# Reordered first loads, a second column of its own, and bias rows in four column groups

## The chip, the cores and the metric

The kernel runs on one core of a Trainium2 chip. The metric is the device time of one execution in microseconds, as the median of several runs. All data are float32. Large products are made of three matmuls each: an operand is split into a high part (rounded for TensorE's float32r) and a low part (the rest), and high x high, low x high and high x low are summed.

## The reference

One transformer block over 1024 tokens of width 1024: an adaptive norm whose shift, scale and gate come from a small vector c, a projection into eight heads of dilated attention and eight heads of a gated delta rule, an output projection, and a gated feed-forward layer. What the change touches is the beginning:

```
c_act = silu(c)
mod = c_act @ w_ada + b_ada                      # 6 x 1024
sh1, sc1, g1, sh2, sc2, g2 = split(mod, 6)
h = rmsnorm(x, norm_attn_g) * (1.0 + sc1) + sh1
proj = h @ w_in                                  # q, k, v, z, b, a
...
bias = rel_bias[bucket(steps * dilation)]        # 32 buckets x 8 heads, added to the attention scores
```

## The kernel before

Channels lie on partitions. The 1024 channels of x are eight blocks of 128 (blocks 0 to 7 here; block 0 is the first); block k of x is `xts[k]`, 128 x 1024 tokens. `mod` is kept as 48 columns of 128: columns 0 to 7 are sh1, columns 8 to 15 are sc1, and so on. The gate of block k is `G1[:, k] = (1 + mod[:, 8+k]) * ga[:, k]`, with ga the norm's weights; so block k of x can only be scaled when column 8+k of mod is known.

The first stage projects x by 512 columns of w_in (`wfirst`), before the norm's division by the root mean square is known; that is multiplied in later. For each block k:

- ScalarE casts the weights `wf[k]` to their high part `wh_f` (L343) and GpSimd makes the low part `wl_f` (L344).
- ScalarE scales x by G1 into the high part `hh[k]`, in two halves of 512 tokens (L359), and VectorE makes the low part `hl[k]` (L360).
- TensorE adds three matmuls of 512 columns for each of six PSUM banks, f0 to f5 (L247): eighteen matmuls for a block. Banks 0 to 3 want the first half of the tokens, 4 and 5 the second.
- For the norm, ScalarE squares x (L303), and TensorE sums the squares in one bank (`sums`, L305) and multiplies x by the scaled columns for beta and a (`wbg`, L295) in another (`sums2`, L309). Both use four groups of 32 output columns, one after the other, so that four small matmuls share the array.

Blocks 0 to 4 go in that order; of blocks 5 to 7 the six banks are finished bank by bank later (`first_end`).

The columns of mod are sums over the eight blocks of c (`rows4`, L206): for each block four calls of TensorE, one for each group of 32 output partitions. VectorE transposes the result (L214) and adds b_ada (L218). Column 8 has a load of its own, `wa8`, in two halves; the others come in groups, `groups = ((9, 3), (12, 4), (0, 4), (4, 4))`: first column and count. Group 0 (columns 9 to 11) is summed in the middle of block 0, after bank 3; group 1 in block 3; groups 2 and 3 after block 4. A group's weights come in four loads into four buffers (tag `qk`), so loads of a group wait until TensorE has read the one before.

The bias rows (L188) are a product of a 33 x 8 matrix (`rb`: the 32 rows of rel_bias and a row of ones) and a 33 x 1344 table of zeros and ones, in three matmuls of 448 columns with 8 output rows, each into a bank of its own; VectorE negates them into `Rs` (L193). They are stored to DRAM much later (L377), and attention reads them there. They are bound to come after the sum of column 8 on TensorE, and block 0 after them.

All loads are issued by SyncE (SP) in one queue, in the order of the program. The vector c (`cc`), rel_bias, the table (two loads), b_ada (`bada`) and the norm's weights (`ga`) are six small loads ahead of x. Instructions of an engine run in the order in which the program's scheduler put them.

## Time and profile before

| | |
|---|---|
| median of three runs | 1336.08 us |
| lowest, highest run | 1334.43, 1340.38 us |
| the profiled execution | 1336.0 us, span 1334.3 us |
| busy share of the span | PE 98%, DVE 63%, ACT 46%, POOL 18% |
| moved by DMA | 236.82 MB, mean 177 GB/s |

In the profile PE is TensorE's matmuls, PEld its weight loads, DVE is VectorE, ACT is ScalarE, POOL is GpSimd and SPq the issuing of loads and stores by SyncE. A row of the timeline has the start and the length in microseconds, the engine, the line of the kernel, the operation, out<-in by the names of the tiles, and the count; in brackets the idle time of the engine before it and what ended that. A float32 matmul is listed as two records, so 32 calls count as 64. Busy times of the stretches are per engine, followed by the granted clock of TensorE, the share of the sixteen DMA engines and the rate.

### The profile page before, as it was taken

The page shows a single profiled execution, that of the slowest core. Times are in us where ns is not written, and L with a number is a line of the kernel's source. Part 1 is how long each engine was busy: PE and PEld are TensorE (multiplying, and loading weights), DVE is VectorE, ACT ScalarE, POOL GpSimd, SP SyncE. Part 2 cuts the span into 40 slices and gives each one's busy share as a digit, 9 for nine tenths or more (in the row PEclk, how much of TensorE's full clock was granted, in tenths as well). Part 3 has the DMA queues.
Part 4 walks back from the last instruction along what each step waited for, and adds up shares of the span by engine and source line. Part 5 has one row for each costly group of instructions (what it writes and reads, how often), then busy time and mean ns, then how long its engine had stood idle before and what let it go on. Part 6 is the DMA issues. An engine that isn't in the chain of part 4 may idle for free.

```text
span 1334.3 us, 25026 instructions
## 1 busy us (share of the span) xinstructions
PE 1306.8 (98%) x9440; PEld 1066.4 (80%) x9440; DVE 836.2 (63%) x1609; ACT 618.6 (46%) x1238; POOL 236.7 (18%) x241
## 2 busy tenths in 40 slices
PE   8999999999999999999999999999999999999997
PEld 5777797889988877677778788888888888888876
DVE  3685775566946122555289967576766676474597
ACT  4397614337232343544487433333333333444555
POOL 2344503334213432343510000000000000000000
PEclk9999999999999999999999999999999999999999
DMA  8625665466452565763744545364445656666685
GB/s 325 224 70 175 180 206 173 135 201 196 131 155 65 138 158 149 214 189 105 235 154 130 169 152 199 108 209 137 158 150 166 213 205 216 227 222 197 201 266 196
DMA packets 188520, 236.82 MB, mean 177 GB/s; under 512 B 48494, under 2 KB 96079, under 8 KB 188400
## 3 DMA queue, kind: packets, MB, share of 16 engines
q1 hardware_dynamic: 181488, 228.94, 54.4%
q10 hardware_dynamic: 6912, 6.29, 1.4%
q8 instruction: 74, 1.21, 0.4%
q14 instruction: 46, 0.38, 0.1%
HBM read 172.37 MB, written 62.92 MB: 176 GB/s over the span
## 4 chain that ended last, share of the span: by engine, by line
PE 77%; DVE 8%; DMA 7%; ACT 3%; issue 2%; POOL 2%; SPq 1%; ACTq 0%; POOLq 0%; DVEq 0%
PE wua L1686 9%; PE wga L1686 9%; PE X L1888 7%; PE wo L592 6%; PE wuc L1686 4%; PE wgc L1686 4%; PE g_a L592 4%; PE Z L1888 4%; PE f L247 2%; PE wgb L1686 2%; PE Y L1888 2%; PE wub L1686 2%; DVE tm L908 2%; DVE tt L912 2%; PE tr L1399 2%
## 5 line engine op out<-in xcount | busy, mean ns | idle before, releaser
L1676 DVE TENSOR_TENSOR wl_db<-wr_db,wh_db 128x512 fp32r<-128x512 f32 x77 | 52.9, 690 | 67.5 <-ACT wh_db L1675 67.2
L1675 ACT CAST wh_db<-wr_db 128x512 fp32r<-128x512 f32 x77 | 47.5, 622 | 87.3 <-PE X L1888 37.8
L1373 DVE CUSTOM_DVE_ANT_0 X<-S,bt 128x128 f32<-128x128 f32 (+7 forms) x64 | 30.9, 517 | 68.9 <-PE S L1368 43.6
L1888 PE MATMUL X<-wl_db,wh_da 128*128 128x512 f32 x160 | 62.4, 390 | 0.3 <-DVE wl_db L1676 0.3
L1888 PE MATMUL X<-wh_db,wl_da 128*128 128x512 f32 x160 | 62.3, 389 | 0.0
L1888 PE MATMUL X<-wh_db,wh_da 128*128 128x512 f32 x160 | 62.3, 389 | 0.0
L1377 ACT ACTIVATE X<-X,sc 128x128 f32<-128x128 f32 (+7 forms) x64 | 37.0, 579 | 41.0 <-DVE sc L1373 40.9
L1676 DVE TENSOR_TENSOR wl_da<-wr_da,wh_da 128x512 fp32r<-128x512 f32 x77 | 52.8, 686 | 2.1 <-ACT wh_da L1675 2.1
L592 PE MATMUL wo<-yh,wh_wo 128*128 128x512 f32 x128 | 53.4, 417 | 0.1
L1675 ACT CAST wh_da<-wr_da 128x512 fp32r<-128x512 f32 x77 | 47.5, 617 | 12.2 <-PE wua L1686 5.8
L1379 POOL TENSOR_SCALAR X<-X,sc 128x128 f32<-128x128 f32 (+7 forms) x64 | 35.8, 567 | 94.3 <-DVE sc L1378 91.8
L592 PE MATMUL g_a<-hh,wh_a 128*128 128x512 f32 x128 | 51.2, 400 | 0.0
L592 PE MATMUL wo<-yh,wl_wo 128*128 128x512 f32 x128 | 51.1, 400 | 0.0
L592 PE MATMUL wo<-yl,wh_wo 128*128 128x512 f32 x128 | 50.8, 397 | 0.3 <-DVE yl L1506 0.3
L592 PE MATMUL g_a<-hl,wh_a 128*128 128x512 f32 x128 | 50.3, 393 | 0.0
L592 PE MATMUL g_a<-hh,wl_a 128*128 128x512 f32 x128 | 50.1, 391 | 0.0
L1675 ACT CAST wh_wg_s<-wg_s 128x512 fp32r<-128x512 f32 x33 | 20.6, 623 | 57.6 <-PE wuc L1686 24.3
L1675 ACT CAST wh_wu_s<-wu_s 128x512 fp32r<-128x512 f32 x33 | 20.4, 621 | 44.1 <-PE wga L1686 17.2
L1675 ACT CAST wh_wg<-wr_wg 128x512 fp32r<-128x512 f32 x31 | 19.2, 622 | 46.5 <-PE wua L1686 18.9
L618 PE MATMUL g_va<-wh_va,hh 128*128 128x256 f32 x128 | 38.2, 298 | 0.0
L618 PE MATMUL g_va<-wl_va,hh 128*128 128x256 f32 x128 | 38.2, 298 | 0.0
L618 PE MATMUL g_va<-wh_va,hl 128*128 128x256 f32 x128 | 37.8, 296 | 0.0
(552 smaller groups left out, 4138.6 us busy)
## 6 DMA issues: line engine op xcount, KB each, us to landing
wm<-in_wada SPq DMA_DIRECT2D x44, 512.0 KB, 4.9
wr_da<-ao_d SPq DMA_DIRECT2D x77, 256.0 KB, 2.8
wr_wu<-in_wu SPq DMA_DIRECT2D x50, 256.0 KB, 2.8
wr_wg<-in_wg SPq DMA_DIRECT2D x48, 256.0 KB, 3.2
ao_d<-a SPq DMA_DIRECT2D x44, 256.0 KB, 2.9
wr_wd<-in_wdn SPq DMA_DIRECT2D x44, 256.0 KB, 2.8
wr_db<-wt_d SPq DMA_DIRECT2D x44, 256.0 KB, 2.6
ao_d<-as SPq DMA_DIRECT2D x33, 256.0 KB, 2.0
```

Source lines behind the costliest of these rows:

```text
L247: nc.tensor.matmul(first[bank], a[:, w0], b[k][:, cs], start=(k == 0 and n_ == 0), stop=(k == KT - 1 and n_ == 2))
L592: last[0] = nc.tensor.matmul(ps, a[:, w0], b[k0 + k4][:, cs], start=(i == 0), stop=(i == n - 1))
L618: last[0] = nc.tensor.matmul(ps[:, :n], a[k][:, ts_], b[:, w0], start=(i == 0), stop=(i == 23))
L908: nc.vector.tensor_tensor(out=tv, in0=bc(nt[:, j, j + 1 : 32], j + 1), in1=tt[:, j, 0 : j + 1].unsqueeze(1).to_broadcast([P, m, j + 1]), o ...
L912: nc.vector.tensor_tensor(out=tt[:, j + 1 : 32, 0 : j + 1], in0=tt[:, j + 1 : 32, 0 : j + 1], in1=tv, op=ALU.add)
L1373: nc.vector.tensor_tensor_reduce(out=x[:, 0:w], in0=pss[e][:, 0:w], in1=bt[:, e, 480 - w : 480], scale=1.0, scalar=3e38, op0=ALU.add, op1= ...
L1377: nc.scalar.activation(x[:, 0:w], x[:, 0:w], AF.Exp, scale=-1.0, bias=sc[:, 0:1], accum_out=sc[:, 2:3])
L1379: nc.gpsimd.tensor_scalar(out=x[:, 0:w], in0=x[:, 0:w], scalar1=sc[:, 3:4], scalar2=0.0, op0=ALU.mult, op1=ALU.add)
L1675: nc.scalar.copy(hi, src)
L1676: (eng or nc.vector).tensor_tensor(out=lo, in0=src, in1=hi.bitcast(F32), op=ALU.subtract)
L1686: nc.tensor.matmul(ps, a[:, w0], b, start=(first and k == 0 and n_ == 0), stop=(k == 3 and n_ == 2), skip_group_check=True,)
L1888: nc.tensor.matmul(bank[b], a[:, ts_], w, start=(first and n_ == 0), stop=(last and n_ == 2), skip_group_check=True,)
```

## The change

The change rewrites the beginning of the first stage:

- b_ada, the norm's weights and c come in one load, `pk` (128 x 64), between the two halves of column 8's weights. The silu reads c from there.
- Then come w of block 0, x of block 0 in two halves of 512 tokens, the weights of column 9 (`wa[1]`, two halves), x and w of block 1, wba, group 0, the table, and from x of block 2 on the rest as before.
- Column 9 is a group of its own (group 4), summed in block 0 after bank 3; group 0 is now columns 10 and 11, in two loads, and is summed in block 1 after bank 2. The scaled columns `wbg` of blocks 0 and 1 are made together, in block 1.
- The bias rows are four matmuls of 336 columns, one in each group of 32 output columns, all in the first 336 columns of the bank `sums2`. One VectorE instruction negates all four, one memset clears the bank again. They stand in block 1, after bank 2, and block 0 no longer waits for them. rel_bias is now part of the table. Four stores take the place of three.
- The table's two tiles move from buffers with the tag `qd` to `kt`.

The core of the diff:

```diff
-    nc.sync.dma_start(cc[:, 0:KT], I["cc"])
-    nc.scalar.activation(cc[:, 0:KT], cc[:, 0:KT], AF.Silu)
-    rb = const([33, 8], "rb")
-    nc.vector.memset(rb[32:33, :], 1.0)
-    tbl = start("tbl", "qd", [33, 896]), start("tbl2", "qd", [33, 448])
-    wa8 = start("wa8", "qk", [P, KT, P])
...
+    pk = const([P, 64], "pk")
+    wa = [start(f"wa{j}", "qk", [P, KT, P]) for j in range(2)]
+    wa_load(0, 0)
+    nc.sync.dma_start(pk, I["pk"])
+    wa_load(0, 1)
+    nc.scalar.activation(cc[:, 0:KT], pk[:, 56:64], AF.Silu)
+    bada, ga = pk[:, 0:48], pk[:, 48:56]
+    tbl = start("tbl", "kt", [33, 672]), start("tbl2", "kt", [33, 704])
...
-    def bias_rows(behind):
-        for j in range(3):
-            n = 448
-            ps = tbank(f"ps_R{j}")
-            with tc.issue_after(behind[0].ins):
-                mm = nc.tensor.matmul(
-                    ps[:8, 0:n], rb, tbl[j // 2][:, n * (j % 2) : n * (j % 2) + n], start=True, stop=True
-                )
-            Rs = start(f"Rs{j}", "tc", [8, HALF])
-            with tc.issue_after(behind[1].ins):
-                nc.vector.tensor_scalar(out=Rs[:, 0:n], in0=ps[:8, 0:n], scalar1=-1.0, scalar2=None, op0=ALU.mult)
-            Rss.append(Rs)
-        return mm
+    Rs = start("Rs", "tc", [P, HALF])
+    def bias_rows():
+        ps = aux2[:, 0:336]
+        for j in range(4):
+            nc.tensor.matmul(
+                ps[32 * j : 32 * j + 32], tbl[1][:, 672:704], tbl[j // 2][:, 336 * (j % 2) : 336 * (j % 2) + 336],
+                start=False, stop=True, skip_group_check=True,
+            )
+        nc.vector.tensor_scalar(out=Rs[:, 0:336], in0=ps, scalar1=-1.0, scalar2=None, op0=ALU.mult)
+        nc.vector.memset(ps, 0.0)
...
-    groups = ((9, 3), (12, 4), (0, 4), (4, 4))
+    groups = ((10, 2), (12, 4), (0, 4), (4, 4), (9, 1))
...
-    x_load(0)
     w_load(0)
+    for hf in range(2):
+        x_load(0, slice(hf * HALF, (hf + 1) * HALF))
+    for i in range(2):
+        wa_load(1, i)
+    x_load(1)
+    w_load(1)
+    nc.sync.dma_start(wba, I["wba"])
     mod_load(0)
-    nc.sync.dma_start(wba, I["wba"])
-    for k in range(1, 4):
+    nc.sync.dma_start(tbl[0], I["tbl"][:, 0:672])
+    nc.sync.dma_start(tbl[1], I["tbl"][:, 672:1376])
+    for k in range(2, 4):
         x_load(k)
         w_load(k)
...
             for bank in range(6):
-                with tc.issue_after(mm.ins) if (k, bank) == (0, 0) else ExitStack():
-                    first_mm(bank, k)
+                first_mm(bank, k)
                 if (k, bank) == (0, 3):
+                    with tc.issue_after(newest[0].ins):
+                        mod_sum(4)
+                if (k, bank) == (1, 0):
+                    scaled(0, 2)
+                if (k, bank) == (1, 2):
+                    bias_rows()
                     mod_sum(0)
```

The queue of SP, from its first load on, before (wa is column 8's weights, xt is x, wf is w, wm is group 0):

```order
L170 DMA wa_121<-in_wa 128x512
L162 DMA cc<-in_cc 128x8
L170 DMA wa_121<-in_wa 128x512
L171 DMA rb<-in_rel 32x8
L173 DMA tbl<-in_tbl 33x896
L173 DMA tbl_120<-in_tbl 33x448
L119 DMA bada<-in_bada 128x48
L119 DMA ga<-in_ga 128x8
L257 DMA xt_154<-in_xT 128x1024
L260 DMA wf_148<-in_wfirst 128x512
L270 DMA wm_0_168<-in_wada 128x2x384
L270 DMA wm_1_170<-in_wada 128x2x384
```

and with the change (wa_116 is column 8, wa_117 column 9; the lines are those of the changed kernel):

```order
L166 DMA wa_116<-in_wa 128x512
L169 DMA pk<-in_pk 128x64
L166 DMA wa_116<-in_wa 128x512
L254 DMA wf_142<-in_wfirst 128x512
L251 DMA xt_148<-in_xT 128x512 x2
L166 DMA wa_117<-in_wa 128x512 x2
L251 DMA xt_149<-in_xT 128x1024
L254 DMA wf_142<-in_wfirst 128x512
L327 DMA wba<-in_wba 128x256
L265 DMA wm_0_168<-in_wada 128x4x256
L265 DMA wm_1_170<-in_wada 128x4x256
L329 DMA tbl<-in_tbl 33x672
```

The first loads of w and x move from ninth and tenth place to fourth to sixth, and x and w of block 1 ahead of group 0; the table moves behind it.

TensorE up to block 0, before (ps_R are the bias rows, f_138 to f_140 the first three banks, hh_93 and hl_101 block 0 of x):

```order
L206 MATMUL sums<-wa_121,cc 32x32 x32
L188 MATMUL ps_R_260<-tbl,rb 8x448
L188 MATMUL ps_R_264<-tbl,rb 8x448
L188 MATMUL ps_R_268<-tbl_120,rb 8x448
L247 MATMUL f_138<-hh_93,wh_f_219 128x512
L247 MATMUL f_139<-hh_93,wh_f_219 128x512
L247 MATMUL f_140<-hh_93,wh_f_219 128x512
L247 MATMUL f_138<-hh_93,wl_f_220 128x512
```

and with the change (f_132 to f_137 are the six banks):

```order
L200 MATMUL sums<-wa_116,cc 32x32 x32
L241 MATMUL f_132<-hh_93,wh_f_216 128x512
L241 MATMUL f_133<-hh_93,wh_f_216 128x512
L241 MATMUL f_134<-hh_93,wh_f_216 128x512
L241 MATMUL f_135<-hh_93,wh_f_216 128x512
L241 MATMUL f_136<-hh_93,wh_f_216 128x512
L241 MATMUL f_137<-hh_93,wh_f_216 128x512
L241 MATMUL f_132<-hh_93,wl_f_217 128x512
```

The bias rows are gone from here, and six high x high matmuls instead of three stand ahead of the first one that wants the low part of the weights.

TensorE in the middle of block 1 with the change (f_134 and f_135 are its third and fourth bank, hh_94 and hl_102 block 1 of x, wm group 0):

```order
L241 MATMUL f_134<-hh_94,wh_f_315 128x512
L241 MATMUL f_134<-hh_94,wl_f_316 128x512
L241 MATMUL f_134<-hl_102,wh_f_315 128x512
L200 MATMUL sums<-wm_0_168,cc 32x64 x16
L200 MATMUL sums<-wm_1_170,cc 32x64 x16
L241 MATMUL f_135<-hh_94,wh_f_315 128x512
L241 MATMUL f_135<-hh_94,wl_f_316 128x512
L184 MATMUL sums_139<-tbl,tbl_123 32x336 x2
L184 MATMUL sums_139<-tbl_123 32x336 x2
L241 MATMUL f_135<-hl_102,wh_f_315 128x512
```

Before, block 1 held projection matmuls alone, and group 0 was summed in block 0, after the fourth bank; that place now has column 9. The order of the instructions behind the first stage is the same, but for some rows of the second projection's beginning.

## The prediction

> **What bounds the kernel now.** I read the page first, then the stretches of the span, then the waits, then the first 60 us in order of time. The page and two stretches (microseconds, then each engine's busy time, the granted TensorE clock, DMA share, GB/s):

> ```profile
> PE 1306.8 (98%) x9440; PEld 1066.4 (80%) x9440; DVE 836.2 (63%) x1609; ACT 618.6 (46%) x1238; POOL 236.7 (18%) x241
> ...
> 0.00:20.00 20.00, 15.59 (x172) 8.36 (x176) 7.97 (x25) 6.29 (x11) 3.13 (x14) 1.00 0.82 295
> 20.00:60.00 40.00, 39.78 (x358) 27.56 (x348) 20.14 (x31) 21.88 (x34) 12.29 (x10) 1.00 0.79 294
> ```

> TensorE is busy 98% of the span and is the bound. It lacks 4.4 us in the first 20 and 0.2 us in the next 40. So the first stage can lose or gain time only up to about 26 us; behind that its matmuls follow one another.

> The opening, in order of time (start, length, engine, line, what; in brackets the idle time before it and its releaser):

> ```profile
> 1.79 0.43 SPq L170 DMA_DIRECT2D wa<-in_wa  x1
> ...
> 3.93 0.21 ACT L163 ACTIVATE cc<-cc 128x8 f32<-128x8 f32 x1 [1.62 <-DMA cc<-in_cc]
> ...
> 3.94 0.43 SPq L119 DMA_DIRECT2D ga<-in_ga  x1
> ...
> 4.19 0.66 PE L206 MATMUL sums<-wa,cc 128*32 128x32 f32 x32 [4.19 <-ACT cc L163]
> 4.41 0.43 SPq L257 DMA_DIRECT2D xt<-in_xT  x1
> ...
> 5.00 0.66 PE L206 MATMUL sums<-wa,cc 128*32 128x32 f32 x32 [0.15 <-DMA wa<-in_wa]
> ...
> 5.59 4.65 PE L188 MATMUL ps_R<-tbl,rb 33*8 33x448 f32 x6
> ...
> 7.15 0.16 DVE L350 SCALAR_TENSOR_TENSOR G<-mod,ga 128x1 f32<-128x1 f32 x1 [0.98 <-DMA ga<-in_ga]
> ...
> 8.41 1.33 ACT L359 ACTIVATE hh<-xt,G 128x512 fp32r<-128x512 f32 x2 [4.27 <-DMA xt<-in_xT]
> ...
> 9.65 0.60 ACT L343 CAST wh_f<-wf 128x512 fp32r<-128x512 f32 x1
> ...
> 10.30 1.65 PE L247 MATMUL f<-hh,wh_f 128*128 128x512 f32 x3
> ```

> The first projection matmul starts at 10.30. Behind it stands a row of waits: the second half of the first column lands at 5.00, ga at 7.15, x of block 0 only at 8.41 (4.0 us after its issue at 4.41, behind six small loads), and ScalarE casts the weights after scaling x. The bias rows' 4.65 us fill a hole in which TensorE has nothing else.

> From there to block 2:

> ```profile
> 13.24 0.63 PE L247 MATMUL f<-hl,wh_f 128*128 128x512 f32 x1
> ...
> 13.66 0.63 PE L247 MATMUL f<-hh,wl_f 128*128 128x512 f32 x1
> ...
> 15.37 0.59 PE L247 MATMUL f<-hl,wh_f 128*128 128x512 f32 x1
> 15.89 1.31 PEld L206 LDWEIGHTS sums<-wm,cc 128*32 128x32 f32 x64 [0.61 <-issue]
> 15.89 1.53 PE L206 MATMUL sums<-wm,cc 128*32 128x96 f32 x64
> ...
> 18.20 1.34 ACT L359 ACTIVATE hh<-xt,G 128x512 fp32r<-128x512 f32 x2 [6.99 <-DVE G L285]
> 18.38 0.39 PE L247 MATMUL f<-hh,wl_f 128*128 128x512 f32 x1
> ...
> 18.61 0.39 PE L247 MATMUL f<-hl,wh_f 128*128 128x512 f32 x1
> ...
> 20.38 0.96 PE L247 MATMUL f<-hh,wh_f 128*128 128x512 f32 x3
> ...
> 25.19 0.64 PE L305 MATMUL sums<-sq,onesr 128*32 128x256 f32 x8
> 25.76 0.50 PE L247 MATMUL f<-hh,wh_f 128*128 128x512 f32 x1
> ...
> 29.75 0.39 PE L247 MATMUL f<-hl,wh_f 128*128 128x512 f32 x1
> 30.07 0.66 PE L305 MATMUL sums<-sq,onesr 128*32 128x256 f32 x8
> 30.53 0.64 PE L309 MATMUL sums<-xt,wbg 128*32 128x256 f32 x8
> ...
> 31.97 0.50 PE L247 MATMUL f<-hh,wh_f 128*128 128x512 f32 x1
> ```

> Matmuls start 0.42 us apart until about 15.8 and 0.23 apart afterwards, though the stretches above grant a clock of 1.00 throughout; I call these cold and warm, by the spacing. Twelve of block 0's eighteen were cold: 12 x 0.20 = 2.4 us. Block 1 starts at 20.38, block 2 at 25.76. This last number is the yardstick: what the change takes off 25.76 it takes off the kernel, if nothing later is fixed in time.

> **The change part by part.**

> *The start.* The queue is now first column (half), small inputs, first column (half), w of block 0, x of block 0 in two halves. The small inputs in one load (pk, 32 KB) take the place of cc, so the silu stays near 3.9 and the column's second half at 5.0. The gate G no longer waits for ga: 5.66 (end of the column sum) plus the transpose, add and G at their lengths gives about 6.3. x decides. Ahead of x's first half lie w0 and itself, 262 KB each, behind a load that lands at 5.0. The rate is bounded by two rows:

> ```profile
> 4.00:8.00 4.00, 3.66 (x68) 1.46 (x69) 1.11 (x5) 0.14 (x1) 0.00 (x0) 1.00 0.71 242
> 8.00:10.00 2.00, 2.00 (x3) 0.17 (x2) 0.61 (x1) 1.59 (x3) 0.00 (x0) 1.00 0.83 240
> 10.00:12.00 2.00, 1.94 (x5) 1.11 (x4) 1.73 (x2) 1.21 (x2) 1.29 (x1) 1.00 0.95 346
> 12.00:14.00 2.00, 2.00 (x5) 1.49 (x5) 0.83 (x2) 0.00 (x0) 0.00 (x0) 1.00 1.08 410
> ```

> At 346 GB/s it lands at 6.5, at 242 at 7.1; I take 6.9, nearer the rate of that time. Half of hh is 1.33/2 = 0.67, so the first projection matmul starts at 7.6, between 7.2 and 8.2 (the upper end allows x half a microsecond beyond the slower rate). The cast of w0 (0.60) now precedes hh and is done by then. GpSimd's wl and VectorE's hl are needed only from the seventh matmul on, 2.5 us later. Gain at the start: 10.30 - 7.6 = 2.7 us.

> *The cold stretch.* In the trace it ended 5.5 us after the first projection matmul, and earlier narrow matmuls from 4.19 on had not ended it. I take the same: twelve cold matmuls, 2.4 us, as before. [...]

> *Column 9 by itself, inside block 0.* Fourteen matmuls, then its 32 calls. The three-column sum held TensorE from about 15.8 to 17.35; at 32 columns of 96 this is 0.43 us of streaming and 0.3 us of changing over, and as much again for the two-column sum: 0.7 here, 1.1 in block 1. Before, it was one sum of 1.55, so splitting costs 0.3 more. After it: 12 cold and two warm matmuls from 7.6 reach 13.2, the sum 13.9. From the end of such a sum (17.42) to hh (18.20) and its first half (18.87) the trace has 1.45 us, so block 1 can start at 15.4. The remaining four matmuls last to 14.8: a wait of 0.6 us (0 if all are cold, 1.0 if x comes late). VectorE scales wba for columns 8 and 9 ahead of hl of block 1; wba is the load after w of block 1 and lands near 13 by the rates above, so it holds nothing up.

> *Bias rows.* They leave the hole and enter block 1. In four column groups a 256-wide sum follows the next after about 0.43 us (rows at 30.07 and 30.53); at 336 wide that is 0.57, and 0.28 for changing over: +0.85 on TensorE (low end 0.57; high end 1.2 if nothing overlaps so well at 336). On VectorE they add one evacuation and one memset, below 0.61 and 0.4 us by these rows:

> ```profile
> 7.29 0.61 DVE L193 TENSOR_SCALAR Rs<-ps_R 8x448 f32<-8x448 f32 x1
> ...
> 50.49 0.27 DVE L405 MEMSET sums<- 128x256 f32 x1
> ```

> The sums of wbg in the same bank wait for that memset. Between bias matmuls and these sums stand seven projection matmuls, 1.6 us, which covers it; uncovered it would cost up to 0.5.

> *Squares.* Those of blocks 0 and 1 follow block 1 together: 1.99 us, as from 29.98 to 31.97. Before, three quarters of them lay between 18.99 and 20.38, and one quarter at 25.19.

> *The sum.* Block 2 starts at 15.4 + 18 x 0.228 (4.1) + 1.1 (two columns) + 0.85 (bias) + 2.0 (squares) = 23.45, against 25.76: 2.3 us earlier. Nothing then stalls block 1. Before, its eighteen matmuls took from 20.38 to 25.19, 4.8 us for 4.1 us of streaming, so 0.7 us went to waits.

> *Loads and queues.* SP's list up to w of block 3 holds the same bytes in another order (column 9 is in a load of its own). Before and now SP refills its buffers as TensorE frees them (waits of the first 60 us as total, times, longest; two issues; a wait of TensorE's weight loads between 60 and 110 us):

> ```profile
> SPq L270 <- PE sums L206: 20.2, 8, 9.9
> SPq L260 <- DMA wm<-in_wada: 3.1, 4, 1.0
> ...
> 33.58 1.92 SPq L270 DMA_DIRECT2D wm<-in_wada  x4
> ...
> 54.22 2.48 SPq L377 DMA_DIRECT2D R_d<-Rs  x3
> ...
> PEld sums L206 <- DMA wm<-in_wada: 0.4, 1, 0.4
> ```

> So later loads move with TensorE, not with the clock on the wall. Four stores of Rs instead of three add 0.83 us to SP; behind them stand gff and the next weights, which are not wanted for 20 us. The table moves behind x of block 1; only the bias rows want it.

> *Against the profiled execution:* 1336.0 (span 1334.3 and 1.7 around it), which is the median of the runs (1336.08). 1336.0 - 2.3 = **1333.7 us**.

> [...]

> **The rivals.**

> *The lead is smaller because the cold stretch stays where it was.* If narrow early work, the bias rows too, helps to end it, then without them it still ends near 15.85. From 7.6 that is 19 cold matmuls, seven more than before, 7 x 0.2 = 1.4 us: 1335.1. For it: the stretch ended 11.7 us after the first matmul of any kind. Against: 4.65 us of bias rows did not end it. Chance 0.15.

> *The cold stretch is shorter.* [...] Chance 0.12. [...]

> *The lead is used up later.* A load bound to arrival could absorb it; the sum of columns 4 to 7 waited 0.4 us for its load around 60 us. Against: those columns' loads start when TensorE frees their buffers. 1336.0, chance 0.08.

> *Slower: the two-column weights arrive late.* They lie behind 2.78 MB, and their sum stands in TensorE's order ahead of nine matmuls of block 1. It is due at 17.5. At 242 GB/s to 10 us and 346 to 410 after, they land at 15.8. The lead is gone when they land 2.3 us late, at 19.8: below 226 GB/s on the mean over 3.83 MB. If their short rows (1 KB) move at half of 242 GB/s and the rest at 242, they land at 23.0, a stall of 5.5 us: 1339.2. For it: ga's 4 KB took 3.2 us (3.94 to 7.15). Against: with 1.5 KB rows in the queue the rate rose to 410 GB/s. Chance 0.07.

> **How the numbers follow.** Forecast 0.55 (ends: start 7.2 to 8.2, bias 0.57 to 1.2, wait 0 to 1.0: 1332.3 to 1335.4), the rivals 0.15, 0.12, 0.08 and 0.07, anything else 0.03. The range reaches past these ends by the scatter of a median of runs that lie between 1334.4 and 1340.4, some 2 us each way: 1330.5 to 1338.0; the late weights and the rest stay outside. About 0.5% (6.7 us) is what a measurement of this kernel can tell from no change. No case reaches it, so most of the chance is "same": faster 0.05, same 0.91, slower 0.04, the outer two for what I have not thought of.

> **What would show it.** Right: first projection matmul at 7.2 to 8.2, spacing falling to 0.23 at about 13, block 1 at 15 to 16, block 2 at 23 to 24 without a wait for DMA, and every later landmark (first sum of squares done, first wo matmul) 2 to 3 us earlier. Wrong: hh of block 0 waiting for x beyond 7.5; a two-column sum that waits for its load; VectorE's memset holding up the wbg sums; or block 2 early and the end not.

## The result

| | us |
|---|---|
| before, median of 13 runs (lowest to highest) | 1336.08 (1334.43 to 1340.38) |
| after, median of 13 runs (lowest to highest) | 1346.96 (1336.02 to 1365.65) |
| ratio, 95% interval | 1.0075 (1.0053 to 1.0098) |
| the profiled execution of after | 1341.12, span 1339.4 |

The changed kernel is slower by 0.75%; 1333.7 was forecast. The ratios, here and below, leave out executions more than 1.5% above the fastest of their kernel (one of after here, 1365.65), so they are not the quotients of the medians beside them. Its runs scatter five times as far as those of before, and with the mean granted clock of TensorE: 1336.02 us at 0.999, 1341.95 at 0.998, 1350.85 at 0.989, 1355.11 at 0.986, 1365.65 at 0.975. Seven of its 13 executions had a clock of 0.992 or less, against two of the 115 executions of the kernel before in the sets below. I call such an execution a low one. The line is drawn by eye: the profiled execution of after, which lost the clock for 13.65 us as told below, has 0.993 and is not counted.

The page of after: the busy time of TensorE is that of before (1306.8), with 66 matmul records more; the granted clock has a dip in the twelfth slice (368 to 402 us). The last row is a DMA queue; on the page of before it has 74 packets.

```profile
span 1339.4 us, 25152 instructions
...
PE 1306.7 (98%) x9506; PEld 1070.1 (80%) x9506; DVE 835.5 (62%) x1610; ACT 618.3 (46%) x1238; POOL 236.5 (18%) x241
...
PEclk9999999999979999999999999999999999999999
...
q8 instruction: 75, 1.23, 0.4%
```

The first stage did nearly what was forecast. In order of time:

```profile
5.88 0.65 PE L200 MATMUL sums<-wa,cc 128*32 128x32 f32 x32 [1.03 <-DMA wa<-in_wa]
...
7.10 0.62 ACT L347 CAST wh_f<-wf 128x512 fp32r<-128x512 f32 x1 [2.95 <-DMA wf<-in_wfirst]
7.81 1.34 ACT L360 ACTIVATE hh<-xt,G 128x512 fp32r<-128x512 f32 x2
8.58 2.93 PE L241 MATMUL f<-hh,wh_f 128*128 128x512 f32 x6 [2.05 <-ACT hh L360]
...
11.73 0.58 PE L241 MATMUL f<-hl,wh_f 128*128 128x512 f32 x1
...
12.38 0.40 PE L241 MATMUL f<-hl,wh_f 128*128 128x512 f32 x1
...
13.61 0.76 PE L200 MATMUL sums<-wa,cc 128*32 128x32 f32 x64
...
15.83 0.50 PE L241 MATMUL f<-hh,wh_f 128*128 128x512 f32 x1 [0.33 <-ACT hh L360]
...
18.09 1.10 PE L200 MATMUL sums<-wm,cc 128*32 128x64 f32 x64
...
22.31 0.66 PE L302 MATMUL sums<-sq,onesr 128*32 128x256 f32 x8
...
24.21 0.50 PE L241 MATMUL f<-hh,wh_f 128*128 128x512 f32 x1
```

The first projection matmul is at 8.58, block 1 at 15.83, block 2 at 24.21 without a wait for a load; before, block 2 started at 25.76. That is a lead of 1.55 us (2.3 was forecast).

Setting each matmul of one trace against the same matmul of the other shows what became of it: the lead is 1.0 us at 100 us and 0.2 us at 378, and at 390 the changed kernel is 6.0 us late. (Part of this is the execution: a second one of the same kernel, a_same below, is 3.0 us ahead at 378, so the place of the loss counts here, not the size.) Between 378 and 390 the rest of a projection (g_va) fills the gaps of the delta rule's chain of narrow matmuls (lv, lw, lx, head by head). The stretches, first of before, then of after (busy times of PE, PEld, DVE, ACT, POOL, then the granted clock):

```profile
376.00:380.00 4.00, 3.38 (x143) 2.70 (x136) 3.05 (x8) 3.52 (x10) 0.00 (x0) 1.00 0.98 287
380.00:384.00 4.00, 4.00 (x49) 3.65 (x48) 2.44 (x5) 1.21 (x4) 1.26 (x2) 1.00 0.69 223
```

```profile
376.00:380.00 4.00, 2.97 (x114) 2.34 (x108) 2.83 (x7) 3.49 (x10) 0.00 (x0) 1.00 0.94 287
380.00:384.00 4.00, 3.73 (x27) 3.38 (x27) 1.84 (x4) 0.37 (x1) 0.95 (x1) 0.59 0.57 196
384.00:388.00 4.00, 4.00 (x81) 3.59 (x81) 0.60 (x2) 1.39 (x3) 0.30 (x1) 0.50 0.13 39
388.00:392.00 4.00, 4.00 (x50) 3.59 (x44) 1.47 (x3) 1.09 (x3) 0.60 (x1) 0.50 0.01 4
```

After has 0.41 us less of TensorE between 376 and 380 and 0.27 us less in the next four, and its clock is halved, for 13.65 us from 380.75 on. The rows just ahead of that, in before and in after:

```profile
379.75 0.28 PE L618 MATMUL g_va<-wh_va,hl 128*128 128x256 f32 x1
379.96 1.14 PE L970 MATMUL lw<-tc,dt 64*64 64x64 f32 x16
```

```profile
379.51 0.28 PE L624 MATMUL g_va<-wh_va,hl 128*128 128x256 f32 x1
379.72 0.13 PEld L976 LDWEIGHTS lw<-tc,dt 64*64 64x64 f32 x1
380.27 1.49 PE L976 MATMUL lw<-tc,dt 64*64 64x64 f32 x16 [0.48 <-ACT U L970]
```

In after TensorE idles 0.48 us ahead of lw. The profile names ScalarE's copy of U, but that is inferred. The wait stands on lw's first weight load, and that load ran at 379.72, before the copy of U named there had ended (379.97); ScalarE's copy of tc, which lw reads, had ended at 379.21. So the wait was over, and a changed order is not at work either: from 75 us on both traces have the same TensorE instructions in the same order, but for two that start within 0.3 us of their neighbours.

### The profile page after: what moved, and what is told of

Read it like the earlier page. It is cut to its first block, busy times and chain, and to the rows that moved or that the text cites. A ratio compares the mean times of both kernels' runs of the same rounds, so it can differ in the third digit from the quotient of the medians.

```text
span 1339.4 us, 25152 instructions
## 1 busy us (share of the span) xinstructions
PE 1306.7 (98%) x9506; PEld 1070.1 (80%) x9506; DVE 835.5 (62%) x1610; ACT 618.3 (46%) x1238; POOL 236.5 (18%) x241
## 3 DMA queue, kind: packets, MB, share of 16 engines
q10 hardware_dynamic: 6912, 6.29, 1.4%
q8 instruction: 75, 1.23, 0.4%
## 4 chain that ended last, share of the span: by engine, by line
PE 77%; DVE 10%; DMA 6%; issue 3%; ACT 2%; POOL 1%; SPq 0%; ACTq 0%; DVEq 0%; POOLq 0%
PE wua L1692 9%; PE wga L1692 9%; PE wo L598 6%; PE X L1894 6%; PE wgc L1692 4%; PE wuc L1692 4%; PE g_a L598 4%; PE f L241 3%; PE Z L1894 3%; PE wgb L1692 2%; PE wub L1692 2%; PE Y L1894 2%; PE g_va L624 2%; DVE tm L914 2%; DVE tt L918 2%
```

## The experiments

Four theories. **A**: the low clock comes in windows of a fixed raster, and an earlier or later start of the later stages shifts where they fall. **B**: one of the changed pieces (the bias rows, where their tiles lie) costs something later. **C**: the chip was disturbed. **D**, formed after the first four runs: TensorE's instructions are fetched in blocks, and the change moves the ends of the blocks.

In all tables of this part "late" is how much later than in before the matmuls near 100 us start, from the matched traces; "low" counts the executions at a clock of 0.992 or less; before is the kernel before on the same chip.

**The changed kernel again (a_same).** No edit. 

> The changed kernel again, unaltered. In its profile the first stage is 1.56 us ahead at block 2, and the loss comes at 380.75 us, where the granted clock is half for 13.65 us. Theory A (the later half-clock stretches depend on how the light stretches of TensorE lie against a 3.41 us raster that is tied to the program's start, and the shift by 1 to 1.5 us has moved them) and theory B (a changed piece makes a later wait longer, whatever the shift): again 5 to 15 us slower than before, with mean clocks of 0.98 to 0.998 that go with the times. Theory C (those runs met a disturbed chip): within 2 us of before.

**The changed kernel, shifted (a_d5), and the kernel before, shifted (b_d10).** Five and ten matmuls repeated at the start of the second projection:

```diff
+                if (k, j, hf) == (0, 0, 0):
+                    for _n in range(5):      # b_d10: 10
+                        nc.tensor.matmul(banks[j], wh[:, w0], hh[k][:, cs], start=True, stop=True)
```

a_d5: 

> The changed kernel with five more matmuls of 512 columns (repeats of the first one of the second projection's first bank, overwritten by the real one) at about 68 us: 5 x 0.228 = 1.1 us more work, which puts everything behind back to where it stood before the change. Theory A: the half-clock stretches go back as well, 1335 to 1339 us, clock 0.995 or more. Theory B: the changed kernel's time plus 1.1 us, with clocks as low as there.

b_d10: 

> The kernel before with ten such matmuls: 2.3 us more work, which on a raster of 3.41 us is the same place as a lead of 1.1 us. Theory A: slower by clearly more than 2.3 us, 1341 to 1350, clock below 0.993. Theory B: 1338.4, clock as before (0.996).

**The bias rows alone (c_bias).** The kernel before with the four-group bias rows in block 1, the table in the buffers kt, four stores, and without `rb`; the scaled columns of blocks 0 to 3 are made in block 1. 

> The kernel before with the bias part of the change alone: four matmuls of 336 columns in column groups in block 1, one evacuation, four stores, the table in the other buffers; loads and columns as before. Block 0 can start no earlier than x allows (hh at 8.41), so the first stage ends within 1 us of before. Theory B with the bias piece as the cause: 1342 to 1350. Theory B with another piece: 1335 to 1338. Theory A: by its shift alone, which I expect within 1 us, 1335 to 1340.

| kernel | us | before | ratio (95%) | late | low |
|---|---|---|---|---|---|
| a_same | 1340.30 | 1335.88 | 1.0058 (1.0027 to 1.0088) | -1.2 | 4 of 12 |
| a_d5 | 1340.30 | 1335.88 | 1.0037 (1.0015 to 1.0058) | 0.2 | 4 of 12 |
| b_d10 | 1339.91 | 1335.88 | 1.0027 (1.0011 to 1.0043) | 3.7 | 0 of 12 |
| c_bias | 1345.79 | 1335.88 | 1.0086 (1.0055 to 1.0118) | 2.9 | 2 of 6 |

C falls: a second set, with before on the same chip, shows the same. A falls as the cause: before shifted by 3.7 us is 4.0 us slower, no more, with no low execution, and the changed kernel shifted back stays slow with as many. B is not refuted. But the profiled execution of a_same, whose clock was full up to 543 us, shows where it loses 2.3 us between 374 and 392:

```profile
375.34 0.21 PE L962 MATMUL lv<-cs,U 32*32 32x32 f32 x1 [0.82 <-DVE cs L958]
...
377.58 1.09 PE L976 MATMUL lw<-tc,dt 64*64 64x64 f32 x16 [0.54 <-ACT U L970]
...
383.13 0.27 PE L976 MATMUL lw<-tc,dt 64*64 64x64 f32 x1
384.28 1.03 PE L976 MATMUL lw<-tc,dt 64*64 64x64 f32 x15 [0.88 <-issue]
```

Of the second lw one matmul runs, TensorE idles 0.88 us, and the other fifteen follow. All sixteen stand together and wait for the same thing; "issue" means that the profile shows nothing that the engine waits for. With the hole ahead of the third lw (0.47 us at 390.64) the three make 1.9 of the 2.3 us. What can be missing between two like matmuls is the instruction itself. The queue "instruction" moves 1.23 MB in 75 packets, 16.4 KB each, and the 19,012 matmuls and weight loads of the page are 74.3 times 256. These are the packets of TensorE's instructions: their number goes with that count from kernel to kernel, from 74 packets for the 18,880 of before to 77 for the 19,524 of g_a128 below. In the stretch from 375.1 to 376.3 of a_same stands one such packet, and one from 381.6 to 383.0; the stretches around them (372.5 to 375.1, 376.3 to 381.7) have none:

```profile
DMA packets 302, 0.36 MB, mean 304 GB/s; under 512 B 32, under 2 KB 230, under 8 KB 301
...
q8 instruction: 1, 0.02, 4.9%
```

```profile
q10 hardware_dynamic: 59, 0.04, 9.5%
q8 instruction: 1, 0.02, 4.9%
q14 instruction: 1, 0.01, 2.1%
```

By their records these two end at 376.15 and 382.89, and the two lw go on at 377.58 and 384.28, 1.4 us later each. Counting TensorE's matmuls, weight loads and semaphore instructions from the start, the last one ahead of the three holes is number 7361, 7617 and 7873: 256 apart, each 193 in its block of 256 (the count leaves out what the trace does not record). 7361 is the weight load of the first lw. In before that load is number 7231, and 7105, which is 193 in its block, is the first matmul of the second burst of lv, ahead of which TensorE waits 0.62 us for VectorE's cs anyway. The change has 33 float32 matmuls more (32 for the second column, one for the bias rows); each is two records and two weight loads, in all 132 instructions: half a block. This is theory D.

**Moving the block ends (e_a64, f_b64, g_a128).** Matmuls of one column, whose result nothing reads, ahead of everything, where TensorE idles for its first inputs; the order of everything else stays:

```diff
+    for _i in range(64):      # f_b64: 64, before; g_a128: 128; i_a32, j_b32: 32; k_a16: 16
+        nc.tensor.matmul(first[5][0:32, 0:1], sh1[:, 0:32], sh1[:, 0:1], start=True, stop=True)
```

e_a64: 

> The changed kernel with 64 matmuls of one column put ahead of everything on TensorE, where it idles for its first inputs; nothing reads what they write, and the order of all other instructions is that of the changed kernel. Theory D (instruction blocks): the trace of the changed kernel shows TensorE's instructions fetched in blocks of 256, and TensorE idle at its instruction 7361, which is 193 in its block of 256, ahead of the third step of the delta rule (lw); 66 added matmuls moved the block's end by 129 from the place in the kernel before where TensorE waits for VectorE anyway (lv after cs). 64 more matmuls are 128 instructions and move it back: no idle time of 0.3 us or over ahead of lw between 370 and 395 us, no run with a clock of 0.992 or less, median 1332.5 to 1336.5, the 1.6 us of the first stage kept or nearly. Theory B (one of the changed pieces, the bias rows or where their tiles lie, costs something later): as the changed kernel, median 1339 to 1342, some runs at 1350 or over.

f_b64: 

> The kernel before with the same 64 matmuls of one column ahead of everything, and nothing else changed. Theory D: the ends of the instruction blocks now lie where they lie in the changed kernel, so TensorE idles 0.4 to 0.9 us ahead of one or more of the four lw between 370 and 395 us, the median is 1338 to 1342, and about one run in three has a clock of 0.992 or less and takes 1348 us or more. Theory B: as the kernel before, median 1335 to 1337, no run with such a clock.

g_a128: 

> The changed kernel with 128 such matmuls ahead of everything: 256 instructions, a whole block. Theory D: block ends fall on the same instructions as in the changed kernel, so it behaves as that one: idle ahead of lw, median 1338 to 1344, about one run in three at a clock of 0.992 or less. A rival to D, that the early matmuls themselves help (TensorE warmed sooner, the raster of the clock shifted): at least as good as with 64. Theory B: as the changed kernel too, so this run tells D from the rival only together with the run with 64.

**Bias rows with their bytes kept (h_cpad).** c_bias with an unused constant of 32 bytes a partition in place of `rb`. 

> The kernel before with the bias rows alone in four column groups in block one, as in the earlier run, but with an unused tile of 32 bytes in each partition in place of the removed constant, so that all later tiles lie where they lay. If the place of the tiles in memory slowed the matmuls of 820 to 1110 us (0.2289 us apart instead of 0.2267): 0.2267 throughout, and a median some 4 us below the earlier 1345.8, that is 1340 to 1343. If not, the spacing and the median stay. Theory D: 2 matmuls more than the kernel before move the block's end by 4 instructions, to the place where TensorE waits for VectorE anyway; little idle time ahead of lw.

| kernel | us | before | ratio (95%) | late | low |
|---|---|---|---|---|---|
| e_a64 | 1348.47 | 1335.31 | 1.0074 (1.0039 to 1.0110) | 2.5 | 6 of 12 |
| f_b64 | 1339.54 | 1335.31 | 1.0034 (1.0013 to 1.0054) | 4.7 | 0 of 12 |
| g_a128 | 1351.46 | 1335.31 | 1.0116 (1.0091 to 1.0140) | 7.9 | 1 of 6 |
| h_cpad | 1338.25 | 1335.31 | 1.0023 (1.0007 to 1.0040) | 3.4 | 0 of 10 |

The expectations for e_a64 and f_b64 rested on a wrong count, and those for g_a128 (1338 to 1344) and h_cpad (1340 to 1343) missed. Each of these matmuls is two records with two weight loads, 127 of them shown in one row (the last one runs among the sums):

```profile
1.48 6.93 PE L230 MATMUL f<-sh 128*32 128x1 f32 x127 [1.48 <-DVE sh L192]
```

So 64 are 256 instructions, a whole block, and moved nothing; 128 are two blocks. Read that way the three are controls that theory D needs: with the block ends of after, idle ahead of lw (0.88 and 0.74 us in e_a64) and low executions; with those of before (f_b64), neither, and a median that is 4.2 us up where the first stage is 4.7 us late. The 54 ns of each record also made the first stage late, in g_a128 by 7.9 us, which is half of its loss. h_cpad is 2.9 us slower where it is 3.4 us late, without a low execution: the bias rows cost what they cost in the first stage and nothing later. B falls for these pieces; what c_bias has beyond h_cpad is told at the end.

**Half a block (i_a32, j_b32).** i_a32: 

> The run with 64 matmuls showed that each of these f32 matmuls is four instructions of TensorE (two passes, each with its weight load), so that 64 of them were a whole block of 256 and left the block ends where they were: lw stayed at 193 in its block, and idle. 32 of them are 128 instructions. The changed kernel with 32: theory D puts lw at 65 in its block and lv after cs at 193, as in the kernel before; so no idle time of 0.3 us or over ahead of lw between 370 and 395 us, no run with a clock of 0.992 or less, and a median of 1333 to 1336.5 (first stage: the 32 end near 5.0 us, ahead of the second half of column 8 at 5.9, and cost nothing or 0.3 us). Theory B: as the changed kernel, median 1339 to 1342 with a third of the runs at 1348 or over.

j_b32: 

> The kernel before with 32 such matmuls ahead of everything (128 instructions). Theory D: lw of the delta rule comes to 192 or 193 in its block as in the changed kernel: TensorE idles 0.2 to 0.9 us ahead of two or more of the four lw between 370 and 395 us, and about one run in three has a clock of 0.992 or less; median 1338 to 1344. The first stage ends 0.5 to 1 us later, since the 32 run to 5.2 us where the sums of column 8 began at 4.2. Theory B: 1336 to 1337.5, and no such clock, as with 64 (1339.5, of which 4.3 us from the first stage).

| kernel | us | before | ratio (95%) | late | low |
|---|---|---|---|---|---|
| i_a32 | 1334.45 | 1338.04 | 0.9974 (0.9955 to 0.9992) | 0.0 | 0 of 12 |
| j_b32 | 1343.90 | 1338.04 | 1.0050 (1.0020 to 1.0080) | 1.6 | 5 of 12 |

Both came as D says. With 32 idle matmuls the changed kernel is 0.26% below before and has no low execution; with the same 32 the kernel before gets the holes in lw and the low executions. First j_b32, second and third lw, then i_a32, second lw:

```profile
389.29 0.33 PE L972 MATMUL lw<-tc,dt 64*64 64x64 f32 x2
390.16 1.02 PE L972 MATMUL lw<-tc,dt 64*64 64x64 f32 x14 [0.55 <-issue]
...
395.99 0.27 PE L972 MATMUL lw<-tc,dt 64*64 64x64 f32 x1
396.52 1.08 PE L972 MATMUL lw<-tc,dt 64*64 64x64 f32 x15 [0.27 <-issue]
```

```profile
385.38 0.28 PE L626 MATMUL g_va<-wh_va,hh 128*128 128x256 f32 x1
385.59 1.14 PE L978 MATMUL lw<-tc,dt 64*64 64x64 f32 x16
```

**Quarters of a block (k_a16, n_a16, l_a48), and 32 better placed (m_a32s).** l_a48 and m_a32s put 16 of theirs behind the sums of column 8, bound to come after the last of them. n_a16 is k_a16 once more.

k_a16: 

> The changed kernel with 16 of the one-column matmuls ahead of everything: 64 instructions, a quarter of a block. Theory D: block ends come to the middle of the second burst of lv (lv after U and cs) of each head, 64 instructions ahead of lw, where nothing covers a late block either: TensorE idles 0.4 us or over inside that burst in two or more heads, and the kernel is no faster than the changed one, 1338 to 1345, with some clocks of 0.992 or less. A rival, that any dummy matmuls at the start help: 1334 to 1336 as with 32.

l_a48: 

> The changed kernel with 32 of them ahead of everything and 16 behind the sums of column 8, where TensorE waits for hh: 192 instructions, three quarters of a block. Theory D: block ends come to the middle of the first burst of lv in the first head and of lx in the next two. The block before the first of them is long (its matmuls are wide), so that the next is there in time; behind it the heads hold 256 instructions each in 6 to 7 us. So less idle time than with 0 or 64, 0 to 0.5 us in all between 370 and 395 us, a median of 1333.5 to 1338, and few or no clocks of 0.992 or less. The rival, that dummies at the start help by themselves: 1334 to 1336.

m_a32s: 

> The changed kernel with 32 of the one-column matmuls, 16 ahead of everything and 16 behind the sums of column 8, both in idle time of TensorE. Theory D: block ends as in the kernel before, so no idle time of 0.3 us or over ahead of or inside lw between 370 and 395 us, no clock of 0.992 or less in most sets of 12, and, since the first stage is as in the run with 48 (block two 1.6 us ahead of the kernel before, where the run with all 32 ahead kept 0.6), 1.0 to 3.0 us below the kernel before of the same chip: a ratio of 0.9975 to 0.9993.

n_a16: 

> The run with 16 matmuls ahead once more, for a profile of another execution. In the first one the load of tn landed 2 us late, the clock fell at 379.9 us and stayed at half for 47.8 us, so that it can't be seen what a block end in the second burst of lv costs at full clock. Theory D: where the clock stays up, a hole of 0.4 us or over inside the second burst of lv (matmuls of the same kind on both sides) in two or more heads. If the bursts run through in 0.7 us as in the kernel before, then with 16 it isn't block ends that cost the time, and theory D covers only ends at lw.

| kernel | us | before | ratio (95%) | late | low |
|---|---|---|---|---|---|
| k_a16 | 1352.47 | 1335.20 | 1.0103 (1.0056 to 1.0150) | -1.2 | 5 of 6 |
| l_a48 | 1336.66 | 1335.20 | 1.0012 (0.9996 to 1.0028) | -1.0 | 0 of 12 |
| m_a32s | 1334.69 | 1336.70 | 0.9989 (0.9974 to 1.0003) | -0.8 | 1 of 12 |
| n_a16 | 1342.76 (one run) | 1336.70 | | | clock 0.992 |

l_a48 has no hole ahead of lw and no low execution. m_a32s is 2.0 us below before, as expected, but its interval still holds no change. So it is not that idle matmuls help: with 16, 64 and 128 the kernel stays slow, 32 and 48 mend it. k_a16 is slow, beyond the 1338 to 1345 that D gave, and not by the hole that D said: neither profile has one of 0.4 us inside the second burst of lv, though in both the clock was at half by then, so what a block end costs there at full clock stays untested. Both have another hole, ahead of the chain's first burst (k_a16, then n_a16):

```profile
372.10 0.37 SPq L925 DMA_DIRECT2D tn<-tn_d  x1
...
377.97 1.78 DVE L953 STREAM_TRANSPOSE U<-tn 32x256 f32<-32x256 f32 x4 [8.54 <-DMA tn<-tn_d]
377.89 1.20 PE L948 MATMUL lv<-tn,dt 32*32 32x32 f32 x64 [1.32 <-DMA tn<-tn_d]
```

```profile
367.86 0.37 SPq L925 DMA_DIRECT2D tn<-tn_d  x1
...
373.72 1.78 DVE L953 STREAM_TRANSPOSE U<-tn 32x256 f32<-32x256 f32 x4 [8.54 <-DMA tn<-tn_d]
373.64 1.20 PE L948 MATMUL lv<-tn,dt 32*32 32x32 f32 x64 [1.14 <-DMA tn<-tn_d]
```

From the issue of tn's load to VectorE's first read are 5.87 and 5.86 us here. In thirteen of the other fourteen traces of this study they are 4.45 to 4.60, in c_bias 5.29. Here alone a fetch of TensorE's instructions falls into that load: in k_a16 between 372.1 and 377.9 there is one, and in before, from 371.1 to 375.6, none:

```profile
DMA packets 4362, 0.78 MB, mean 134 GB/s; under 512 B 4128, under 2 KB 4361, under 8 KB 4361
...
q8 instruction: 1, 0.02, 1.0%
```

```profile
DMA packets 4373, 0.77 MB, mean 170 GB/s; under 512 B 4138, under 2 KB 4373, under 8 KB 4373
```

It fits that the fetch, a transfer like others, held up the load; two executions show both together, but no run parts the one from the other, and c_bias has part of the delay without a fetch, so this is argued and not shown. In both the clock then fell, for 47.8 us in k_a16 and 17.1 us in n_a16.

**A second place.** The traces have the same thing at some 540 us, where ScalarE waits for a load from DRAM (ydr) and TensorE then for et, which ScalarE copies behind it. First before, then a_same:

```profile
541.57 1.63 PE L1429 MATMUL y<-et,va 128*64 128x128 f32 x25 [0.31 <-ACT et L1403]
```

```profile
540.98 0.72 ACT L1511 ACTIVATE yh<-ydr,ngc 128x512 fp32r<-128x512 f32 x1 [4.08 <-DMA ydr<-yd_d]
...
543.37 2.82 PE L1435 MATMUL y<-et,va 128*64 128x128 f32 x25 [3.10 <-ACT et L1409]
```

In the six traces with the block ends of after, or ten instructions beside them (after, a_same, a_d5, e_a64, g_a128, j_b32), a fetch of TensorE's instructions falls into the issue or the flight of that load, and TensorE waits 0.89 to 3.10 us for et; in the other ten none does, and the wait is 0.27 to 0.73 us. In a_same, e_a64 and j_b32 (1.93 us and over) the clock fell for 3.41 us behind it. So lw is not the only place where the block ends cost time; that the fetch is what delays the load is argued here too.

**All sets together.** Of the executions of these six kernels, 27 of 67 are low; of those with the block ends of before or some twenty instructions beside them (f_b64, b_d10, c_bias, h_cpad, i_a32, m_a32s), 3 of 64, and 2 of the 115 of the kernel before itself.

## Why the prediction was wrong

*The start, 2.7 us gained: 1.7.* w of block 0 landed at 7.1, not x at 6.9, and its cast (0.62) stands ahead of hh on ScalarE. I had it "done by then". The second half of column 8 landed 0.9 us later than before, behind pk.

*The cold stretch, 5.5 us: 3.5.* The rival with the shorter stretch came true: the records of the clock begin at 12.12, and there the spacing fell from 0.42 to 0.23 us. It did not come of the change: a_same, the same kernel, has 2.8 us, and i_a32 and m_a32s, which run the same block 0, 5.2 and 5.3. Over the sixteen traces it is 2.8 to 6.2 us, so that what after gained here was luck. What ends the stretch, no run shows.

*Column 9, bias rows, squares.* 0.76 us for 0.7, 0.80 for 0.85 (from 19.46 to 20.49, less one matmul), 1.90 for 1.99; the two-column sum (1.10 for 1.1) did not wait for its load. (No run shows the 0.28 to 0.3 us of changing over, which the sum holds for each of these, by itself. In after the sum of column 9 starts 0.32 us after the matmul ahead of it, and behind the sum the second matmul 0.33 us after the first, where others follow after 0.23.) Block 2 at 24.21 for 23.45: 0.43 of that is block 1's start, 15.83 for 15.4.

*The step that failed* is the sentence behind the yardstick: "what the change takes off 25.76 it takes off the kernel, if nothing later is fixed in time". I looked for what is fixed in time and found only loads. What is fixed is the number of an instruction: the ends of TensorE's blocks of 256, which 132 more instructions moved from a place where TensorE waits anyway into lw. There the late block costs 0.2 to 0.9 us up to three times (1.9 us in a_same), and with it the mean clock falls to 0.992 or less in a third to a half of the executions (after, a_same, e_a64, j_b32), whose median is 13 to 18 us above that of the others of their kernel. Those others are not free of loss either: in after their median is 1341.1. The rival "the lead is used up later" came nearest, but with a load that absorbs the lead and no more (1336.0, chance 0.08); nothing in the sum had a price for 33 more matmuls beyond their time.

*With the block ends moved back* the loss is gone, and the forecast is within the scatter, but not shown: against before of their chips l_a48 is 1.5 us above, m_a32s 2.0 and i_a32 3.6 below, where 2.3 was forecast. Only i_a32 is clear of no change (0.9974, 0.9955 to 0.9992), and it has no lead at 100 us (0.0), so that its 3.6 us do not come from the first stage. Before was slowest on its chip (1338.04; 1335.2 to 1336.7 on the others).

*Why some executions keep the clock up in lw's holes* can be seen in part. In all sixteen traces the clock changes only at steps of 3.413 us, counted from the first record of the clock, and every half-clock stretch that ends inside the span lasts a multiple of it: 3.413 in before, 13.65 in after (four times), 17.1 in n_a16 (five) and 47.8 in k_a16 (fourteen). In after it fell at 251.05 and at 380.75, 70 and 108 steps from 12.12. The last of these, 377.34 to 380.75, holds both the wait ahead of lv's second burst and the hole ahead of lw, 1.23 us of idle time together, and at its end the clock fell. In a_same a step ends between the two (376.37), so that they count 0.82 and 0.54, and the clock stayed. In this chain all four traces with a step of 0.93 us idle or more lost the clock at its end (g_a128 0.93, after 1.23, k_a16 1.37, n_a16 1.44), and the twelve with 0.88 or less kept it. Where the steps lie differs from execution to execution (they begin at 11.14 in a_same and 12.12 in after), so part of this is chance. No run varied it alone, so this is a pattern of the traces and not an experiment.

*Open:* what starts a fetch, and why c_bias, with the block ends of before, had two low executions of six.

## What to carry to other kernels

When a small change early in a long program makes a late, unchanged stage slower, compare the stage's rows in both traces and look for idle time between like matmuls, put down to "issue": here that was a late block of instructions. Count the instructions of the engine up to there, and add some where it idles, by a quarter of a block at a time, and see whether the holes move. This is cheap, not free: 32 idle matmuls ahead of everything took 1.0 us of the first stage's lead, 64 took 3.5. Here it mattered where many short instructions run one after the other in a chain, 256 of them in 4.2 to 6.0 us.

## What the runs showed of the hardware

```profile
L1682 PE MATMUL wga<-H11h,wh_wg 128*128 128x512 f32 x28 | 11.1, 396 | 0.0
```

```profile
L1684 PE MATMUL wga<-H11h,wh_wg 128*128 128x512 f32 x28 | 10.9, 389 | 0.0
```

  In the matched traces this made c_bias some 3 us later between 790 and 1110 us; its median is 9.9 us above before of its chip, that of h_cpad 2.9, and the low executions are a part of that.
